# Block inverse of a delta-rule kernel: an order for its four float16 conversions on ScalarE

## The chip, the cores and the metric

The kernel runs on one core of a Trainium2 chip. The time is the device time of one execution in microseconds, from the first to the last instruction with what the launch adds around it; the numbers of a comparison are medians of several runs. A core has TensorE for matrix products (PE in the profile), VectorE (DVE), ScalarE (ACT), GpSimd (POOL), and SyncE (SP), which issues transfers. ScalarE and GpSimd issue transfers too, each from its own queue (ACTq, POOL).

## The reference

One inference step of a mixer with three branches (a bidirectional gated DeltaNet, a spatial-gating MLP, a Fourier mixer) over 128 context tokens and 2048 latent tokens. What matters here is the DeltaNet. Cut to that:

```python
m = eye + bc[..., :, None] * jnp.einsum('bnhik,bnhjk->bnhij', kc, kc) * dec_strict
rhs = jnp.concatenate([vc * bc[..., None], kc * (bc * jnp.exp(gam))[..., None]], axis=-1)
sol = lax.linalg.triangular_solve(m, rhs, left_side=True, lower=True, unit_diagonal=True)
u0, w = sol[..., :DV], sol[..., DV:]
...
def step(s, inp):
    u0_, w_, qk_, qg_, kd_, gl_ = inp
    u = u0_ - jnp.einsum('bhck,bhkv->bhcv', w_, s)
    o = jnp.einsum('bhck,bhkv->bhcv', qg_, s) + jnp.einsum('bhij,bhjv->bhiv', qk_, u)
    s = gl_[..., None, None] * s + jnp.einsum('bhck,bhcv->bhkv', kd_, u)
    return s, o
```

The matrix m of each chunk is triangular with ones on its diagonal. The kernel inverts it: 32 by 32 blocks on the diagonal first (the block inverse), and from them larger blocks by products.

## The kernel before, in words

The tokens lie in 17 chunks of 128 (chunk 16 is the context). PE's products are made of float16 pairs, a high and a low half of each operand, hence three products for one. Wherever a float32 tile becomes such a pair, ScalarE writes the high half (a Copy with a scale) and VectorE the low half (scaled value minus high half).

Two streams of work are written into one another. The main stream goes through the branches' projections, gates and mixers and gives PE most of its work. The second stream is a Python generator, `delta()`, which the main stream steps along by `pace.tick` and `pace.part` (lines 410 to 450): one step for each 1.6 us of the main stream's matrix work. `delta()` first prepares all chunks and makes the block inverses, then runs the scan, the serial part over 2 x 17 chunks.

The preparation, `prep` (line 1007), goes through seven steps for each chunk: keys made unit length (sums of squares on ScalarE, L1022), queries (L1041) and values (L1036), the transposed keys T (L1050), two steps with the products of keys (L1064 to L1069), two with the products of queries and keys (L1080 to L1083). Each step that makes a float16 tile hands its store to `late` (line 988), which issues it from ScalarE's queue one such step afterwards (L998). `late` also issues, with each such step, one transfer from the list `extra` (L1003).

The chunks form five groups: chunk 16 alone, then four groups of four. `base_inverse(g)` (line 1092) inverts the 32 by 32 blocks of a whole group at once, in one tile with the blocks on the partitions. It is stepped after each preparation step of the following group, so that inverse g runs beside the preparation of group g + 1; the fifth runs alone, after all preparation. It loads the blocks (L1103) into the two halves X and tmp of the tile XB, runs 31 elimination steps that alternate between VectorE (L1114) and GpSimd (L1115) on the tile E, and then writes the result as float16 pairs back into XB, in four parts: two halves j0 of the columns, each in two layouts w. For each part there is one conversion on ScalarE (L1122), the low half on VectorE (L1123) and a `yield`. After each half its two stores to memory (tensor `ei`) follow: in the first four inverses they are put on the list `extra`, so that `late` issues them from ScalarE's queue (two that are left after the fourth go to SP's, L1431); in the fifth one goes to SP's queue (L1130) and one to ScalarE's (L1131).

With eight empty steps at its beginning and fifteen for the elimination, the four conversions of inverses one to four are written behind the third, fourth, fifth and sixth step of the last chunk of the group in preparation, with the main stream's instructions between them as its pace brings it.

The scan's `level` loads `ei` (L1171) and other tiles (L1175, L1177), and its first product is PE's first on the tiles ES and N. The tiles of the scan take the place of the tiles of the preparation in on-chip memory (`dl.close()`, then a new pool), so that they can be written only once the last stores out of XB have landed.

The order of the instructions on each engine is not the written order. It is planned when the kernel is built: a list scheduler goes through the instructions by a model of their times and lets each engine take what is ready. The hardware then runs each engine's list in that order. Where the written code wants a certain order, it says `issue_after(ins)`: the instructions in that block come behind `ins` in their engine's list. This is an order only, with no semaphore. `queued()` of the engine wrapper does this with the newest instruction that has been written so far for that engine; transfers that the engine issues count among them. Before the change it is used in two places, both on VectorE (L1106 and L1356):

```python
def queued(self):
    e = self.engine.engine
    newest = next((i for i in reversed(self.tc.nc.cur_bb.bb.instructions) if i.engine == e), None)
    return ExitStack() if newest is None else self.tc.issue_after(newest)
```

Of the kernel before, what the change touches and what calls it, by code (L numbers as in the profile page):

```python
# [14 lines left out]
AF = mybir.ActivationFunctionType  # L15
# [20 lines left out]
FS = 4096.0  # L36
# [158 lines left out]
def hybrid_flow_kernel(ctx: ExitStack, tc: tile.TileContext, x_prompt, x_sample, state_delta, c, c_ctx, w_ada,  # L195
# [4 lines left out]
    G, V, A, PE = [_InTurn(tc, e_) for e_ in (nc.gpsimd, nc.vector, nc.scalar, nc.tensor)]  # L200
# [9 lines left out]
    def sb(pl, shape, tag, dt=F32, bufs=None):  # L210
        kw = {} if bufs is None else {"bufs": bufs}
        return pl.tile(list(shape), dt, tag=tag, name=nm(tag), **kw)
# [190 lines left out]
    def getw(n=1, ahead=0):  # L403
        i = wnext[0]
        wnext[0] += n
        fetch(i + n)
        while len(wdone) - len(wsteps) < i + n:
            weight_step()
        fetch(i + n + ahead)
        r = wdone[i:i + n]  # L410
        return r[0] if n == 1 else r
# [519 lines left out]
    for ct in range(12):  # L931
        w = getw(1, 2 if ct < 6 else min(4, 15 - ct))
# [159 lines left out]
    def base_inverse(g):  # L1092
        nt = len(GROUPS[g])
        nb = 16 * nt
        XB = sb(dq, [P, 2048], "XB")
        X, tmp = XB[:, 0:1024], XB[:, 1024:2048]
        E = sb(dq, [P, 1024], "E")
        if nt < 4:
            V.memset(X, 0.0)
            V.memset(tmp, 0.0)  # L1100
        b3 = lambda t_: t_.rearrange("p (j i) -> p j i", j=32)
        for d in range(2):
            SY.dma_start((X if d == 0 else tmp)[64 * d:64 * d + nb, :], ndD[g][d].rearrange("t h (b j) i -> (t h b) (j i)", b=4))  # L1103
        for _ in range(8):
            yield 0
        with V.queued():  # L1106
            V.tensor_copy(b3(X[64:P, :]), tmp[64:P, :].rearrange("p (i j) -> p j i", j=32))
        G.memset(E, 0.0)
        G.memset(E[:, 0:1024:33], 1.0)
        X3, E3 = b3(X), b3(E)  # L1110
        for k in range(31, 0, -1):
            n_ = 32 - k
            t3 = tmp[:, 0:k * n_].rearrange("p (j i) -> p j i", j=k)
            V.tensor_tensor(t3, X3[:, 0:k, k:k + 1].to_broadcast([P, k, n_]), E3[:, k:k + 1, k:32].to_broadcast([P, k, n_]), ALU.mult)  # L1114
            G.tensor_tensor(E3[:, 0:k, k:32], E3[:, 0:k, k:32], t3, ALU.subtract)  # L1115
            if k % 2 == 0:
                yield 1
        both = XB.bitcast(F16).rearrange("p (j l w c) -> p j l w c", j=32, l=2, w=2)
        for j0 in (0, 16):
            js = slice(j0, j0 + 16)  # L1120
            for w, src in ((0, E3), (1, E.rearrange("p (i j) -> p j i", j=32))):
                A.activation(both[:, js, 0, w, :], src[:, js], AF.Copy, scale=FS)  # L1122
                V.scalar_tensor_tensor(both[:, js, 1, w, :], src[:, js], FS, both[:, js, 0, w, :], ALU.mult, ALU.subtract)  # L1123
                yield 1
            out = [(eD[g][d][js].rearrange("j t (y x) -> (t y) j x", x=128),
                    both[64 * d:64 * d + nb, js].rearrange("p j l w c -> p j (l w c)")) for d in range(2)]
            if g < 4:
                extra.extend(out)
            else:
                SY.dma_start(*out[0])  # L1130
                A.dma_start(*out[1])  # L1131
# [278 lines left out]
    def delta():  # L1410
# [5 lines left out]
        for i_, (g, ci, t) in enumerate(seq):  # L1416
            if ci == 0 and g:
                for r_ in base:
                    if r_:
                        yield 1  # L1420
                base = base_inverse(g - 1)
            for n_, _ in enumerate(prep(g, ci, t, seq[i_ + 1][2] if i_ < 16 else None, held)):
                yield 1
                if next(base, 0):
                    yield 1
# [6 lines left out]
        for _ in base_inverse(4):  # L1432
            yield 1
# [757 lines left out]
```

## Time and profile before

| | |
|---|---|
| median of 3 runs | 2145.91 us (2145.07 to 2146.69) |
| the profiled execution | 2150.07 us |
| its span, first to last instruction | 2148.3 us |
| mean granted clock of TensorE | 0.992 |
| PE busy | 2085.2 us (97%) |
| ScalarE busy | 1060.8 us (49%) |
| VectorE busy | 1327.9 us (62%) |
| GpSimd busy | 843.3 us (39%) |

A row of a timeline gives the start in us from the span's start, the time it took, the engine, the line, the operation, the tiles (written<-read) and how many instructions are merged into the row; in square brackets stands how long the engine was idle before it and what ended that. A row of the chain gives start, time and what the chain went through. A row of stretches gives the stretch, its length, the busy time of PE, PE's weight loads, VectorE, ScalarE and GpSimd with the number of instructions, then the granted clock (1.00 is full), the share of the DMA engines and GB/s. ACTq and SPq are instructions that the engine only issues or waits in, such as DMA issues.

### The profile page before, as it was taken

The numbers are of one execution on the slowest core, as the hardware profiler recorded it, in microseconds if no ns is written. First come the engines' busy times: TensorE is split into PE (matmuls) and PEld (weight loads), VectorE is DVE, ScalarE is ACT, GpSimd is POOL, SyncE is SP. The second block draws the span as 40 slices with busy tenths as digits, with TensorE's granted clock in tenths as the row PEclk, the third lists the DMA queues.
The fourth block names the chain that finished last, engine by engine and source line by source line (L and its number), as shares of the span: only waits on it lengthen the run. The fifth ranks groups of instructions, "written<-read, shape, count | busy, mean of one in ns | idle before, by whom it ended". The sixth has DMA issues, their size and how long they took to land.

```text
span 2148.3 us, 42630 instructions
## 1 busy us (share of the span) xinstructions
PE 2085.2 (97%) x16133; PEld 1196.8 (56%) x16133; DVE 1327.9 (62%) x2945; ACT 1060.8 (49%) x2457; POOL 843.3 (39%) x1089
## 2 busy tenths in 40 slices
PE   7999999999999999989899999999999999999997
PEld 4454444455555677777555556565655444444443
DVE  6656854388777786456655555766665564666245
ACT  5554744475656664445544445665653353453112
POOL 0321332225565555542321233354542234333464
PEclk9999999999999999999999999999999999999999
DMA  9525722277877743444655555867664655456852
GB/s 353 219 77 189 267 102 102 74 223 226 259 228 246 225 138 93 121 132 138 205 182 161 167 162 184 258 206 232 210 204 127 209 167 173 167 198 240 335 220 89
DMA packets 222910, 403.25 MB, mean 188 GB/s; under 512 B 39720, under 2 KB 109632, under 8 KB 219888
## 3 DMA queue, kind: packets, MB, share of 16 engines
q1 hardware_dynamic: 167664, 290.84, 42.5%
q0 software_dynamic: 15216, 65.89, 8.2%
q10 hardware_dynamic: 39824, 43.79, 6.0%
q8 instruction: 127, 2.08, 0.4%
q14 instruction: 79, 0.65, 0.1%
HBM read 258.19 MB, written 142.24 MB: 186 GB/s over the span
## 4 chain that ended last, share of the span: by engine, by line
PE 70%; DVE 9%; DMA 9%; ACT 4%; POOL 4%; issue 3%; SPq 1%; ACTq 0%; DVEq 0%; POOLq 0%
PE b L250 66%; PE b L182 4%; DMA st<-br 2%; POOL E L1115 1%; DMA pa<-pa 1%; DMA wst<-in_w_blk_dram 1%; DVE XB L1114 1%; POOL st L1466 1%; DMA ab<-in_w_adb_dram 1%; PE b L1016 1%; DMA sqk<-qk 1%; DMA ei<-XB 0%; ACT xh L182 0%; ACT nd L1066 0%; DVE XB L1123 0%
## 5 line engine op out<-in xcount | busy, mean ns | idle before, releaser
L250 PE MATMUL b<-xh,whi 128*128 128x512 f16 (+1 forms) x1920 | 651.1, 348 | 2.8 <-DVE sg L1456 1.8
L250 PE MATMUL b<-xl,whi 128*128 128x512 f16 (+1 forms) x1920 | 651.2, 348 | 0.0
L250 PE MATMUL b<-xh,wlo 128*128 128x512 f16 (+1 forms) x1920 | 650.1, 347 | 0.0
L250 PEld LDWEIGHTS <-whi 128*128 128x128 f16 x3856 | 352.7, 98 | 326.4 <-issue 7.3
L250 PEld LDWEIGHTS <-wlo 128*128 128x128 f16 x1928 | 188.8, 98 | 176.1 <-issue 2.2
L250 PE MATMUL b<-big,bhi 128*128 128x512 f16 (+1 forms) x960 | 252.3, 347 | 1.9 <-ACT big L1699 1.1
L250 PE MATMUL b<-big,blo 128*128 128x512 f16 (+1 forms) x480 | 163.1, 347 | 0.0
L1743 POOL TENSOR_TENSOR mrow<-mrow,sg 128x512 f32<-128x512 f32 (+1 forms) x80 | 94.4, 1182 | 131.2 <-DVE sg L1742 99.5
L953 POOL TENSOR_TENSOR cy<-cy,raw 128x545 f32<-128x545 f32 (+1 forms) x48 | 65.8, 1395 | 181.8 <-ACT raw L952 181.8
L250 PEld LDWEIGHTS <-xh 128*128 128x128 f16 x1496 | 116.9, 98 | 28.8 <-issue 1.4
L250 PEld LDWEIGHTS <-bhi 128*128 128x128 f16 x960 | 87.7, 98 | 78.1 <-issue 2.6
L1115 POOL TENSOR_TENSOR E<-E,XB 128x31 f32<-128x31 f32 (+15 forms) x155 | 94.1, 607 | 85.7 <-DVE XB L1114 68.8
L250 PEld LDWEIGHTS <-xl 128*128 128x128 f16 x1068 | 98.1, 98 | 44.8 <-DMA tw<-tw 1.4
L1733 ACT ACTIVATE sg<-b,winv 128x512 f32<-128x512 f32 (+1 forms) x120 | 73.9, 616 | 87.1 <-PE b L250 86.4
L1188 POOL COPY T<-ES 32x256 f16<-32x256 f16 x68 | 31.8, 467 | 188.6 <-DMA ES<-ei 167.9
L250 PE MATMUL b<-whi,xh 128*128 128x128 f16 x544 | 92.8, 219 | 0.0
L250 PE MATMUL b<-whi,xl 128*128 128x128 f16 x544 | 92.8, 219 | 0.0
L250 PE MATMUL b<-wlo,xh 128*128 128x128 f16 x544 | 92.8, 219 | 0.0
L328 DVE SCALAR_TENSOR_TENSOR wlo<-wst,wsc,whi 128x1024 f16<-128x1024 f32 x52 | 71.1, 1368 | 33.1 <-ACT whi L327 32.7
L315 ACT ACTIVATE wlo<-wst 128x1024 f16<-128x1024 f32 x52 | 54.9, 1055 | 54.5 <-DMA wst<-in_w_blk_dram 51.2
L1114 DVE TENSOR_TENSOR XB<-XB,E 128x31 f32<-128x31 f32 (+15 forms) x155 | 55.2, 356 | 41.8 <-POOL E L1115 41.2
L1295 POOL TENSOR_TENSOR skn<-skn,ed 128x512 f32<-128x512 f32 x34 | 37.7, 1109 | 109.7 <-DMA skn<-kv 109.7
(532 smaller groups left out, 4317.9 us busy)
## 6 DMA issues: line engine op xcount, KB each, us to landing
wst<-in_w_blk_dram SPq DMA_DIRECT2D x58, 512.0 KB, 4.5
pa<-pa POOLq DMA_DIRECT2D x16, 896.0 KB, 4.4
qkv<-cy POOLq DMA_DIRECT2D x12, 1089.0 KB, 5.3
st<-br SPq DMA_DIRECT2D x48, 256.0 KB, 3.2
mrow<-mrg SPq DMA_DIRECT2D x16, 576.0 KB, 4.6
pa<-pa SPq DMA_DIRECT2D x5, 1792.0 KB, 17.3
dc<-dec SPq DMA_DIRECT2D x17, 512.0 KB, 4.8
kq<-qkv SPq DMA_DIRECT2D x34, 256.0 KB, 4.5
```

The costliest lines, as they stand in the source:

```text
L182: self.last = f(*args, **kw)
L250: newest[0] = PE.matmul(out, l, r, start=start, stop=stop, skip_group_check=reopened)
L315: w.squared = A.activation(w.lo, st, AF.Square, accum_out=ss)
L328: w.low = V.scalar_tensor_tensor(w.lo, st, s, w.hi, ALU.mult, ALU.subtract)
L953: G.tensor_tensor(y[:, c0:c1], y[:, c0:c1], raw[:, 1 + c0:1 + c1], ALU.mult)
L1016: PE.transpose(ps[:, hs(h)], cur[part][:, h, :], ident)
L1114: V.tensor_tensor(t3, X3[:, 0:k, k:k + 1].to_broadcast([P, k, n_]), E3[:, k:k + 1, k:32].to_broadcast([P, k, n_]), ALU.mult)
L1115: G.tensor_tensor(E3[:, 0:k, k:32], E3[:, 0:k, k:32], t3, ALU.subtract)
L1188: G.tensor_copy(T16[rows(a0, b), :, :, b], ES[0:32, :, 2 * a0 + b, :, wT])
L1295: G.tensor_tensor(h3(kn_), h3(kn_), bc(ed[:, d, t, :], P), ALU.mult)
L1733: gated_[0] = A.activation(sg, ps, AF.Sigmoid, scale=gw.inv)
L1743: G.tensor_tensor(mr, mr, sg, ALU.add)
```

## The change

Each of the four conversions is put under `A.queued()`: it comes behind the newest instruction written for ScalarE at that point. Nothing is added to or taken from the work.

```diff
@@ -1119,7 +1119,8 @@
         for j0 in (0, 16):
             js = slice(j0, j0 + 16)
             for w, src in ((0, E3), (1, E.rearrange("p (i j) -> p j i", j=32))):
-                A.activation(both[:, js, 0, w, :], src[:, js], AF.Copy, scale=FS)
+                with A.queued():
+                    A.activation(both[:, js, 0, w, :], src[:, js], AF.Copy, scale=FS)
                 V.scalar_tensor_tensor(both[:, js, 1, w, :], src[:, js], FS, both[:, js, 0, w, :], ALU.mult, ALU.subtract)
                 yield 1
```

## The prediction

> **What bounds the kernel now.** I read the page's busy shares first, then the chain of waits piece by piece around the block inverses, then ScalarE's and VectorE's timelines at each inverse, and last the busy time by stretch. Of the page:
>
> ```profile
> span 2148.3 us, 42630 instructions
> PE 2085.2 (97%) x16133; PEld 1196.8 (56%) x16133; DVE 1327.9 (62%) x2945; ACT 1060.8 (49%) x2457; POOL 843.3 (39%) x1089
> ```
>
> TensorE (PE) is busy 2085 of 2148 us, so a change on ScalarE (ACT, 49%) counts only where PE stands still, or where it runs at a lower clock. The line of the diff runs twenty times, and each conversion is followed by its low half on VectorE (DVE):
>
> ```profile
> L1122 ACT ACTIVATE XB<-E x20: 612/846/1112, 548.1 to 881.0; 128x512 f16<-128x512 f32 x20
> L1123 DVE SCALAR_TENSOR_TENSOR XB<-E,XB x20: 671/1031/1485, 552.4 to 882.3; 128x512 f16<-128x512 f32 x20
> ```
>
> That is five inverses of four conversions: 20 x 0.85 = 17 us of ACT in all. No instruction and no byte is added or removed; what moves is the order. Where this order lies on the path is told by the pieces of the chain between the fourth inverse and the first product of the scan:
>
> ```profile
> 817.72 2.03 ACT XB L1122 x3
> 819.77 2.78 DVE XB L1123 x3
> ...
> 823.32 5.18 DMA ei<-XB
> ...
> 829.29 5.19 DMA XB<-nd
> ...
> 874.28 2.37 DMA br<-st
> ...
> 879.10 1.52 ACT XB L1122 x2
> ...
> 883.33 5.41 DMA ei<-XB
> ...
> 899.12 1.72 DMA N<-n
> ```
>
> The reader is to see one serial line: conversions of the fourth inverse, their stores, the loads of the fifth inverse into the same tile, its 31 elimination steps, its conversions, its stores, and then the loads that the scan starts with. At the end of it PE stands and waits, and the stretch behind it is the poorest one of the middle of the run (PE's row, then the stretches: wall time, PE busy, ..., granted clock):
>
> ```profile
> 901.10 0.18 PE L250 MATMUL b<-ES,N 128*128 128x32 f16 x1 [1.95 <-DMA N<-n]
> ```
>
> ```profile
> 895.00:901.00 6.00, 3.72 (x30) 1.87 (x27) 4.43 (x12) 4.47 (x9) 2.54 (x4) 1.00 0.58 154
> 901.00:907.00 6.00, 5.90 (x29) 2.71 (x30) 1.60 (x4) 1.82 (x4) 3.64 (x6) 0.72 0.53 169
> 907.00:914.00 7.00, 4.46 (x28) 1.99 (x27) 2.15 (x5) 1.37 (x4) 1.98 (x4) 1.00 0.27 83
> 914.00:925.00 11.00, 9.51 (x103) 7.64 (x104) 7.01 (x19) 5.02 (x14) 4.47 (x11) 0.69 0.28 79
> 925.00:940.00 15.00, 12.74 (x202) 10.86 (x199) 10.24 (x25) 7.61 (x21) 5.37 (x10) 1.00 0.58 161
> ```
>
> Idle: 2.28 + 0.10 + 2.54 + 1.49 + 2.26 = 8.67 us. Lost to the clock: 6 x 0.28 + 11 x 0.31 = 1.7 + 3.4 = 5.1 us. So 13.8 us of these 45 are not work.
>
> **Which conversions move at all.** In the written order the conversions stand behind the third, fourth, fifth and sixth step of the preparation of a group's last chunk. The new edge makes each wait its turn behind the newest ScalarE instruction written before it, a DMA issue on that queue included. In inverses one to four the first three conversions already run long after those instructions (in the first, all of that chunk's preparation on ScalarE is done before 548). So three of four edges hold already and cost nothing. The edge that bites is the fourth conversion's: in inverses one to three the newest instruction is the issue of the first half's store (L1003), in the fourth it is the square of the 128-token unit (L1467), and in the fifth it is the store L1131 already for the third. A store of the first half is issued only when the second low half is done, so ScalarE now waits for VectorE between conversions.
>
> **Inverses one to three.** The timelines of ScalarE, then VectorE for the first, then ScalarE for the second and third, then the stretches of the latter two:
>
> ```profile
> 548.06 3.09 ACT L1122 ACTIVATE XB<-E 128x512 f16<-128x512 f32 x4 [0.53 <-POOL E L1115]
> ...
> 554.85 2.54 ACTq L1003 DMA_DIRECT2D ei<-XB  x3
> 557.43 0.60 ACT L1050 ACTIVATE T<-b 128x512 f16<-128x512 f32 x1 [3.36 <-DVE XB L1123]
> ```
>
> ```profile
> 555.40 1.65 DVE L1123 SCALAR_TENSOR_TENSOR XB<-E,XB 128x512 f16<-128x512 f32 x2
> ```
>
> ```profile
> 632.47 1.63 ACT L1122 ACTIVATE XB<-E 128x512 f16<-128x512 f32 x2
> 633.69 0.67 ACTq L1003 DMA_DIRECT2D ei<-XB  x1
> ```
>
> ```profile
> 721.68 1.61 ACT L1122 ACTIVATE XB<-E 128x512 f16<-128x512 f32 x2
> 723.88 0.66 ACTq L1003 DMA_DIRECT2D ei<-XB  x1
> ```
>
> ```profile
> 625.00:650.00 25.00, 25.00 (x192) 15.14 (x190) 17.29 (x40) 17.56 (x50) 10.59 (x17) 1.00 0.86 253
> 710.00:735.00 25.00, 25.00 (x145) 13.08 (x143) 17.60 (x39) 15.07 (x42) 12.40 (x20) 1.00 0.69 214
> ```
>
> First: the conversion goes behind the issue at 554.85. With 0.67 us for the issue (the second's row) and 0.61 for the conversion (the shortest of L1122) it ends at 556.13, and its low half (0.67 to 1.03) at 556.8 to 557.2, against 555.40 + 1.65 = 557.05 now. The conversion T, which waits 3.36 us behind the stores in ScalarE's queue, and PE's products of T behind it, come 0.25 us earlier to 0.5 us later (0.15, and 0.35 more if an eviction gets in between). I take +0.2. Second and third: the fourth conversion slips from an end at 634.10 to 634.97 (633.69 + 0.67 + 0.61), and from 723.29 to 725.15: 0.9 and 1.9 us. Behind it wait its low half and the second half's stores, which nobody reads before the scan. PE is busy 25.00 of 25.00 us in both stretches, and this covers it: 0, and at worst these 0.9 + 1.9 us if the cover were gone.
>
> **Inverse four.** ScalarE, then VectorE:
>
> ```profile
> 817.61 3.11 ACT L1122 ACTIVATE XB<-E 128x512 f16<-128x512 f32 x4
> 820.63 0.62 ACT L1467 ACTIVATE sg<-st 128x512 f32<-128x512 f32 x1
> ...
> 821.24 0.29 ACT L1467 ACTIVATE sg<-st 128x128 f32<-128x128 f32 x1
> ```
>
> ```profile
> 818.36 4.18 DVE L1123 SCALAR_TENSOR_TENSOR XB<-E,XB 128x512 f16<-128x512 f32 x4
> ```
>
> Four low halves in 4.18 us are 1.05 each, so the fourth starts at 821.49. The conversion now goes behind both squares. If these move up into its place (0.7 us earlier), it ends at 821.5 and VectorE loses nothing. If they can't, it starts at 821.53, ends at 822.14, and the low half is 0.65 late. The store, the load of the fifth inverse and its 31 steps follow; a step late in these steps can vanish in the wait for the store at 874.28, on which GpSimd's work beside the steps hangs. Between 0 and 0.65, I take 0.3.
>
> **Inverse five.** ScalarE, then VectorE:
>
> ```profile
> 879.00 3.12 ACT L1122 ACTIVATE XB<-E 128x512 f16<-128x512 f32 x4
> 881.72 0.60 ACTq L1131 DMA_DIRECT2D ei<-XB  x1
> 882.02 0.57 ACT L1571 ACTIVATE xc<-b 128x512 f16<-128x512 f32 x1
> ```
>
> ```profile
> 880.63 1.65 DVE L1123 SCALAR_TENSOR_TENSOR XB<-E,XB 128x512 f16<-128x512 f32 x2 [0.30 <-ACT XB L1122]
> ```
>
> The second low half ends at 880.63 + 0.83 = 881.46 and the store is issued at 881.72. Now two conversions stand behind it: 881.72 + 0.60 + 2 x 0.61 = 883.54, then the fourth low half at 0.67 to 1.03, so the second store leaves at 884.2 to 884.6, not 883.33: 0.9 to 1.2 us late. If the eviction xc (0.57) also gets in between, up to 1.8. I take 1.4. Nothing hides it. The scan's tiles lie where the store reads, so GpSimd clears them only then:
>
> ```profile
> 889.13 0.95 POOL L1137 MEMSET R<- 128x1024 f16 x1 [9.39 <-DMA ei<-XB]
> ```
>
> The loads and PE at 901.10 hang on the same end, and PE's gap of 1.95 grows to about 3.6 with the fourth inverse's share.
>
> **The clock behind the gap.** The shown stretches price it: after 1.95 us of idling PE loses 1.7 us to the clock (901 to 907), after the 2.54 us that stand idle in 907 to 914 it loses 3.4. A gap of 3.6 is nearest to the second, so 3.4 - 1.7 = +1.7; the bounds are 0 and 3.4. [...]
>
> **The sum.** 0.2 + 0.3 + 1.4 + 1.7 = +3.6 us. The profiled execution took 2150.07 us, 1.8 more than its span, and is 4.2 above the median of the shown runs; on the profile's own base the new time is 2153.7, and against the median 2145.91 + 3.6 = 2149.5. The lower bounds add up to -0.25 + 0.9 = +0.65, the upper ones to 0.5 + 2.8 (cover gone) + 0.65 + 1.8 + 3.4 = +9.15: 2146.6 to 2155.1.
>
> **The rivals.**
> 1. *Nothing bites.* Three edges in four hold already, and the rest is hidden: PE's order is drawn up anew at the build, with main products put into the gap at 901. For it: PE's 25.00 of 25.00 in two of the five places. Against it: the fifth inverse's store, which has no cover in the trace. Time 2145.9, at most 1.5 off.
> 2. *Faster: the later start is filled.* The order of every engine behind 821 is planned anew with later inputs, and main products go where PE now idles between 895 and 940. There are 13.8 us there; half of it is 6.9, less the 1.9 us of delay: -5.0, so 2140.9. For it: PE waits there for loads (1.95 on N) while another stage has matrix products in hand. Against it: nothing in the edit asks for it, and the planner had the same chance before. It decides if PE's gap before the first product of the scan goes below 1 us.
> 3. *Slower: the scan is what sets the end.* The same planning puts one more product group ahead of the scan's first one. Such a group is 24 products of 512 columns, and the spacing of their starts is (550.22 - 549.14) / 5 = 0.216 us, from the first and the last of six in a row:
>
> ```profile
> 549.14 0.38 PE L250 MATMUL b<-xl,whi 128*128 128x512 f16 x1
> ...
> 550.22 0.38 PE L250 MATMUL b<-xh,whi 128*128 128x512 f16 x1
> ```
>
> So 5.2 us. The scan then starts 1.7 + 5.2 = 6.9 us later and, being serial, ends as much later; where the last branch waits for it this is paid in full: 2152.8. For it: in the stretches from 895 to 940 PE already waits for the scan's steps. Against it: a later stretch in which PE hardly waits:
>
> ```profile
> 1100.00:1300.00 200.00, 199.57 (x1833) 119.27 (x1832) 108.51 (x293) 88.10 (x206) 53.13 (x86) 1.00 0.54 165
> ```
>
> It decides when the last scan tile comes after the products that can be done without it.
>
> **How the numbers follow.** Two measurements of this kernel can be told apart from about 0.2%, or 4.3 us: faster is below 2141.6, slower above 2150.2. The forecast has 0.45; its own range, 2147 to 2152, is cut by the upper bound, 0.25 of it to "same" and 0.20 to "slower". Rival 1 has 0.10, all "same". Rival 2 has 0.23, and rival 3 has 0.22. That gives faster 0.23, same 0.35, slower 0.42. The range goes from 2140 to 2157: down to rival 2's time, and up past the bounds' 2155 by rival 3 with part of the clock's price.
>
> **What would show it.** Right: in the first four inverses three conversions in a row and the fourth behind a store or a square; in the fifth L1131 between the second and third; its second store at 884.2 to 885.2 after a start as now; PE's gap before the first product of ES and N at 3 to 4 us; a clock below 0.72 in the six us behind it. Wrong: that gap at 2 us or less, or gone; conversions spread over the preparation's steps (then the written order is not where I put it); a difference of more than 3 us that arises before 800, where I have only 0.2; or PE's idle time behind 940 changed by more than the sum.

## The result and the profile after

The changed kernel takes 2152.79 us (median; 2150.82 to 2154.68), the kernel before in the same comparison 2145.74 (2140.25 to 2148.55). The ratio is 1.0033, with a 95% interval of 1.0022 to 1.0045: 7.1 us slower, between 4.7 and 9.7. The forecast was 2149.5, in a range of 2140 to 2157.

The two profiled executions must be read with care. That of before took 2150.07 us, more than any of its runs in this comparison; that of after took 2150.84, near its own lowest. They differ by 0.8 us where the medians differ by 7. So the totals of the two profiles can't be subtracted. What can be compared is the order of instructions, single waits, and distances from a fixed point.

In the changed kernel every line behind 1121 has a number higher by one: the conversion is L1123, its low half L1124, the fifth inverse's stores L1131 and L1132, the main stream's conversions L1572 and L1573. The experiments keep the numbers of before.

The page after:

```profile
span 2149.1 us, 42632 instructions
PE 2088.6 (97%) x16133; PEld 1199.8 (56%) x16133; DVE 1331.9 (62%) x2945; ACT 1062.0 (49%) x2457; POOL 843.0 (39%) x1089
```

ScalarE's timeline after, at the first, second and third inverse:

```profile
548.03 2.12 ACT L1123 ACTIVATE XB<-E 128x512 f16<-128x512 f32 x3 [0.53 <-POOL E L1115]
...
554.80 0.33 ACTq L1003 DMA_DIRECT2D ei<-XB  x1
...
555.18 1.08 ACT L1123 ACTIVATE XB<-E 128x512 f16<-128x512 f32 x1 [1.14 <-DVE XB L1124]
...
557.73 0.60 ACT L1050 ACTIVATE T<-b 128x512 f16<-128x512 f32 x1 [1.47 <-DVE XB L1124]
...
634.87 1.10 ACT L1123 ACTIVATE XB<-E 128x512 f16<-128x512 f32 x1
...
723.58 1.34 ACTq L1003 DMA_DIRECT2D ei<-XB  x2
...
724.56 1.10 ACT L1123 ACTIVATE XB<-E 128x512 f16<-128x512 f32 x1
```

Three conversions run at once and the fourth waits behind an issue of a store, as forecast. The conversion T starts at 557.73 instead of 557.43, 0.3 us late; the fourth conversions of the other two now stand at 634.87 and 724.56.

At the fourth and the fifth inverse, ScalarE's timeline, then VectorE's, then SyncE's:

```profile
810.00 1.15 ACT L1123 ACTIVATE XB<-E 128x512 f16<-128x512 f32 x2
...
816.00 1.05 ACT L1123 ACTIVATE XB<-E 128x512 f16<-128x512 f32 x1
816.95 0.58 ACT L1572 ACTIVATE xc<-b 128x512 f16<-128x512 f32 x1
818.14 2.45 ACTq L1003 DMA_DIRECT2D ei<-XB  x2
820.63 0.63 ACT L1468 ACTIVATE sg<-st 128x512 f32<-128x512 f32 x1 [3.10 <-issue]
...
821.55 1.07 ACT L1123 ACTIVATE XB<-E 128x512 f16<-128x512 f32 x1
...
878.57 1.62 ACT L1123 ACTIVATE XB<-E 128x512 f16<-128x512 f32 x2
...
881.96 0.61 ACTq L1132 DMA_DIRECT2D ei<-XB  x1
882.62 1.62 ACT L1123 ACTIVATE XB<-E 128x512 f16<-128x512 f32 x2 [1.06 <-DVE XB L1124]
...
885.34 0.59 ACTq L1132 DMA_DIRECT2D ei<-XB  x1
```

```profile
822.66 1.05 DVE L1124 SCALAR_TENSOR_TENSOR XB<-E,XB 128x512 f16<-128x512 f32 x1 [3.96 <-ACT XB L1123]
...
884.26 1.04 DVE L1124 SCALAR_TENSOR_TENSOR XB<-E,XB 128x512 f16<-128x512 f32 x1 [0.29 <-ACT XB L1123]
```

```profile
823.74 1.37 SPq L1432 DMA_DIRECT2D ei<-XB  x2
```

In the fifth, L1132 (formerly L1131) stands between the second and the third conversion, and the second store is issued at 885.34 instead of 883.33. In the fourth the new order goes further than forecast. The first three conversions no longer stand in a row: two run at 810.00, the third at 816.00. Two issues of stores hold ScalarE's queue for 2.45 us from 818.14, the squares L1468 stand behind them, and the last conversion stands behind both. Its low half starts at 822.66; in before it started at 821.49.

PE, at its first product on ES and N, and as a fixed point ahead of the fourth inverse's conversions the transposes L1049 of the preparation's last chunk but one (after):

```profile
767.77 0.61 PE L1049 MATMUL b<-cst,tok 128*128 128x128 f32 x4
...
902.27 0.18 PE L250 MATMUL b<-ES,N 128*128 128x32 f16 x1 [2.55 <-POOL T L1189]
```

The gap ahead of the scan has grown from 1.95 to 2.55 us, not to 3.6, and its start from 901.10 to 902.27. The six microseconds behind it ran at full clock (a stretch of after):

```profile
901.00:907.00 6.00, 4.73 (x36) 2.52 (x37) 3.35 (x8) 2.94 (x5) 3.50 (x7) 1.00 0.48 124
```

And there is a wait of PE that the forecast doesn't have. ScalarE's timeline after, then VectorE's and PE's, at the load of the fifth inverse:

```profile
827.72 0.60 ACT L1572 ACTIVATE xc<-b 128x512 f16<-128x512 f32 x1 [1.51 <-PE b L250]
```

```profile
834.18 1.03 DVE L1107 COPY XB<-XB 64x1024 f32<-64x1024 f32 x1 [6.65 <-DMA XB<-nd]
835.24 0.69 DVE L1573 SCALAR_TENSOR_TENSOR xc<-b,xc 128x512 f16<-128x512 f32 x1
```

```profile
835.99 0.77 PE L250 MATMUL b<-cf,xc 128*128 128x128 f16 x10 [2.23 <-DVE xc L1573]
```

VectorE stands idle for 6.65 us in front of the copy L1107, which opens the fifth inverse and waits for its load. Behind the copy in VectorE's list stands the low half of a tile of the main stream, xc, and PE waits for that. ScalarE had begun the high half of this tile at 827.72, so what keeps the low half is its place in the list. In the kernel before, it stands ahead of the copy:

```profile
829.16 0.69 DVE L1572 SCALAR_TENSOR_TENSOR xc<-b,xc 128x512 f16<-128x512 f32 x1 [1.87 <-ACT xc L1571]
829.83 0.69 DVE L1572 SCALAR_TENSOR_TENSOR Y<-b,Y 128x512 f16<-128x512 f32 x1
834.50 1.05 DVE L1107 COPY XB<-XB 64x1024 f32<-64x1024 f32 x1 [3.97 <-DMA XB<-nd]
```

The copy waits there too, but what PE wants next is done before it. The stretches around this place, of before and then of after, say what this costs in these two executions:

```profile
768.00:828.00 60.00, 56.55 (x675) 44.40 (x674) 46.68 (x114) 35.24 (x92) 33.95 (x54) 0.97 0.40 126
828.00:836.00 8.00, 8.00 (x147) 8.00 (x145) 2.62 (x4) 2.39 (x4) 0.07 (x1) 1.00 0.49 136
836.00:844.00 8.00, 8.00 (x56) 4.20 (x54) 5.44 (x20) 3.63 (x6) 4.07 (x10) 1.00 0.00 1
844.00:860.00 16.00, 14.87 (x142) 9.61 (x141) 12.18 (x28) 5.02 (x14) 10.71 (x17) 1.00 0.10 34
```

```profile
768.00:828.00 60.00, 57.45 (x689) 45.13 (x688) 47.09 (x113) 35.22 (x92) 34.45 (x52) 0.97 0.41 125
828.00:836.00 8.00, 5.77 (x105) 5.60 (x102) 1.79 (x4) 1.51 (x3) 0.00 (x0) 1.00 0.52 136
836.00:844.00 8.00, 8.00 (x65) 5.75 (x66) 4.36 (x14) 2.51 (x5) 3.94 (x9) 0.79 0.01 3
844.00:860.00 16.00, 15.90 (x124) 9.21 (x122) 12.24 (x31) 5.74 (x13) 9.85 (x16) 1.00 0.11 34
```

From 828 to 844 PE was busy throughout at full clock; now it idles 2.23 us and then loses 8 x 0.21 = 1.7 to the clock. The stretches on both sides give 0.90 and 1.03 of idle time back. Net: 2.0 us lost ahead of the fifth inverse's end, in a stretch from which the forecast took nothing but its 0.3 for a late load.

### The profile page after: what moved, and what is told of

Same layout as the page of the kernel before. It is cut to its first block, busy times and chain, and to the rows that moved or that the text cites. A ratio compares the mean times of both kernels' runs of the same rounds, so it can differ in the third digit from the quotient of the medians.

```text
span 2149.1 us, 42632 instructions
## 1 busy us (share of the span) xinstructions
PE 2088.6 (97%) x16133; PEld 1199.8 (56%) x16133; DVE 1331.9 (62%) x2945; ACT 1062.0 (49%) x2457; POOL 843.0 (39%) x1089
## 4 chain that ended last, share of the span: by engine, by line
PE 45%; DMA 7%; DVE 7%; ACT 3%; POOL 3%; issue 2%; SPq 0%; ACTq 0%; POOLq 0%; DVEq 0%
PE b L250 44%; DMA st<-br 2%; DMA pa<-pa 1%; POOL E L1115 1%; DMA wst<-in_w_blk_dram 1%; DVE XB L1114 1%; POOL st L1467 0%; DMA ei<-XB 0%; DMA ES<-ei 0%; DVE sg L476 0%; ACT of L1376 0%; ACT big L1700 0%; DMA wst<-in_w_ada_dram 0%; DVE big L1701 0%; PE b L1383 0%
```

## The experiments

Two theories stood against each other. The first is that of the forecast: a chain of late stores (inverses four and five), paid at the start of the scan. The second: the edges make the planner draw up the rest of the program anew, and the loss lies in the new order, wherever it is worst. All experiments are the kernel before with the edit in some of the five inverses (g = 0 to 4), or with one thing more. All ratios stand against the kernel before on the same chip (one chip for e1 to e4, one for e5 to e8, one for e9 to e12), with 95% intervals. They are not the quotients of the two medians, which lie up to 0.0013 away (e9: 1.0032).

| run | edges in inverses | ratio | interval | median us, before |
|---|---|---|---|---|
| e1 | all but each one's last (fifth: last two) | 0.9999 | 0.9989 to 1.0009 | 2147.38, 2147.43 |
| e8 | one | 0.9994 | 0.9982 to 1.0007 | 2146.98, 2146.88 |
| e7 | two | 1.0003 | 0.9992 to 1.0015 | 2148.50, 2146.88 |
| e3 | three | 1.0002 | 0.9992 to 1.0011 | 2146.84, 2147.43 |
| e2 | four, five | 1.0000 | 0.9989 to 1.0011 | 2148.25, 2147.43 |
| e6 | one to three | 1.0012 | 1.0000 to 1.0024 | 2148.03, 2146.88 |
| e4 | all but three | 1.0016 | 1.0005 to 1.0027 | 2150.14, 2147.43 |
| e9 | three to five | 1.0019 | 1.0008 to 1.0031 | 2152.34, 2145.51 |
| e5 | all (the change again) | 1.0024 | 1.0014 to 1.0033 | 2151.65, 2146.88 |
| e10 | all, fifth's copy L1107 on GpSimd | 1.0005 | 0.9993 to 1.0017 | 2148.18, 2145.51 |
| e11 | none, fifth's copy L1107 on GpSimd | 0.9993 | 0.9981 to 1.0005 | 2145.58, 2145.51 |
| e12 | none, last conversion of the fifth nine times | 1.0045 | 1.0032 to 1.0058 | 2155.96, 2145.51 |

**Which edges do anything.**

```diff
-A.activation(both[:, js, 0, w, :], src[:, js], AF.Copy, scale=FS)
+with A.queued() if (g < 4 and (j0, w) != (16, 1)) or (g == 4 and j0 == 0) else ExitStack(): A.activation(both[:, js, 0, w, :], src[:, js], AF.Copy, scale=FS)
```

> The order is asked only of the first three conversions of inverses one to four and of the first two of the fifth. Set side by side, every engine's list is that of the kernel before, instruction for instruction. Both theories (late stores of inverses four and five; a new plan behind inverse three): ratio 1.000, inside +-0.1%, about 2146 us. Anything beyond that is what two loadings of one program differ by, and the scale for the other runs. Its profile is a second execution of the plan before: the stall before 550 to 553 us and the wait before the scan's first product stay, the clock's half-speed pieces may fall elsewhere.

The lists of instructions of all five engines are those of the kernel before, and the trace has each engine's instructions in the same order; the time is the same: 0.9999. These fourteen of the twenty edges do nothing. The whole change is in six: the last conversion of each inverse, and in the fifth the one before it too. This run also gives a second profile of the old order, and its span is 2143.1 us, 5.2 shorter than that of before with the same lists.

**One part at a time.** The conditions are `g == 0`, `g == 1`, `g == 2` and `g > 2`:

```diff
-A.activation(both[:, js, 0, w, :], src[:, js], AF.Copy, scale=FS)
+with A.queued() if g > 2 else ExitStack(): A.activation(both[:, js, 0, w, :], src[:, js], AF.Copy, scale=FS)
```

> The order is asked in inverse one alone. Only ScalarE's list differs, in 12 lines: the fourth conversion goes behind the first two stores. If the local wait carries it: the values' and keys' next steps start 0.3 us or more later and the ratio is 1.0005 to 1.002. As predicted: +0.2 us, ratio 0.9995 to 1.0005.

> The order is asked in inverse two alone; PE's list differs in 259 lines between 630 and 760 us. If inverse two carries what all but three showed: ratio 1.001 to 1.0025. If not: 0.999 to 1.001, and inverse one is left.

> The order is asked in inverse three alone; the lists of all engines differ from before in many places behind it (PE 2256 lines). Theory 1: PE is fully busy around this inverse, so nothing, ratio 0.999 to 1.001. Theory 2: the new plan carries the change, ratio 1.002 to 1.0045, +4 to +9 us, with a stall of PE between 800 and 900 us that before does not have.

> The order is asked in inverses four and five alone; PE's list differs from before in 24 lines. Theory 1 (late stores, as predicted): the first product on ES and N comes 1 to 2 us later than before, gap 3 us, and the time carries nearly all of the change, +4 to +7 us, ratio 1.002 to 1.0033. Theory 2 (the plan behind inverse three): the same 1 to 2 us later start, but the time is only +1 to +2 us, ratio below 1.001.

No part alone can be told from the kernel before: each interval holds 1 and reaches 1.5 to 4 us to either side. Both theories miss here: the first expected at least 1.002 of e2, the second of e3. The lists of instructions tell more than the times. The edge in inverse one alone moves 12 lines of ScalarE's list and nothing else. That in two changes 259 lines of PE's list, those in four and five 24. The single edge in inverse three changes 2256 lines: one conversion that comes 2 us later there makes the planner order the rest of the preparation anew, and the scan's beginning too. Compared place by place in the traces, PE's products in after differ from those in before at 1083 places between 643 and 1088 us, and 806 of these lie behind 900 (one product moved shifts all up to its new place). With the late stores of four and five alone the scan does start later (below), and yet this costs too little to be seen in that run.

**Several parts together.** The conditions are `g < 3`, `g != 2`, `g > 1` and, for the change again, `True`:

```diff
-A.activation(both[:, js, 0, w, :], src[:, js], AF.Copy, scale=FS)
+with A.queued() if g > 1 else ExitStack(): A.activation(both[:, js, 0, w, :], src[:, js], AF.Copy, scale=FS)
```

> The order is asked in inverses one to three, where the prediction saw +0.2 us. Additive parts: as all but three less four and five plus three, ratio 1.001 to 1.002. Theory 1 (late stores of four and five): ratio 0.999 to 1.001. Theory 2 (a stall that comes only with all): ratio 0.999 to 1.001, no stall at 834.

> The order is asked in all inverses but the third; PE's list differs from before in 283 lines. Theory 1: as the change, ratio 1.002 to 1.004. Theory 2: as inverses four and five alone, ratio below 1.001, and no stall of PE at 834 us.

> The order is asked in inverses three, four and five. PE's list is that of the whole change but for 259 lines around inverse two. By the profiles so far (nothing lost before 768 us, 7 us between 768 and 972 in the whole change, 3 to 4 in the parts): ratio 1.002 to 1.0033, the stall at 834 us again, the first product on ES and N 2 us late against a fixed point before inverse four. By adding up the times of the parts measured so far (some 2 us from one and two, 1 from three, 2 from four and five): ratio 1.0005 to 1.0018.

> The change itself once more, with its two lines on one, beside the other parts of this call. If the first comparison's +0.33% stands: ratio 1.0022 to 1.0045. If it was high by chance (the parts so far give 0.00% for inverses four and five, 0.02% for three, 0.16% for all but three): ratio 1.0005 to 1.002. Theory 2, a stall of its own at 834 us that only the whole change has: the profile shows it again, 2 us, with a piece of half clock behind it.

The change again is slower again, by 1.0024, or 3.0 to 7.1 us. Inverses three to five give 1.0019 of it; PE's list there differs from that of the whole change only in the 259 lines of inverse two. All but three give 1.0016, one to three 1.0012. So no single edge carries the loss: each combination shows a part of it, and within these intervals (2 us and more to each side) the parts may add up or not. That three to five carry most of it is the best reading of e9, but e4 and e6 keep it from being all.

The traces of the three profiled executions with the new order (after, e5, e9) agree on two places, and the old order's don't have the first. PE's timeline in e5, then in e9, at 834:

```profile
836.61 1.25 PE L250 MATMUL b<-cf,xc 128*128 128x128 f16 x10 [2.68 <-DVE xc L1572]
```

```profile
835.55 0.85 PE L250 MATMUL b<-cf,xc 128*128 128x128 f16 x10 [2.28 <-DVE xc L1572]
```

The stall behind the copy stands in all three, with 2.23 to 2.68 us. It isn't in before, e1 or e8, and not in e2, e4 or e7. In e3 and e6 there are shorter ones (1.42 us; 1.47 and 1.41). So it comes with the new order behind inverse three, and has its full length with the edges of four and five besides.

The other place is the start of the scan. From the transposes L1049 at 768 (767.93 in before, 767.77 in after) to the first product on ES and N it is 133.2 us in before, 132.2 in e1, 132.3 in e7 (whose products behind 713 us stand in the old order) and 131.2 in e8; with the new order it is 134.5 in after, 134.6 in e5 and 134.4 in e9. The means are 132.2 and 134.5: 2.3 us later. With the edges of four and five alone, in e2 and e4, it is 133.9 and 133.6.

**What a late start costs.** To price it by itself, the last conversion of the fifth inverse is run nine times in the kernel before (each time with the same values), which delays its second store and nothing ahead of it:

```diff
-A.activation(both[:, js, 0, w, :], src[:, js], AF.Copy, scale=FS)
+for _ in range(9 if g == 4 and (j0, w) == (16, 1) else 1): A.activation(both[:, js, 0, w, :], src[:, js], AF.Copy, scale=FS)
```

> The kernel before, with the last conversion of inverse five written nine times (the same values; ScalarE does eight more conversions, about 8 x 0.6 = 4.9 us, ahead of the last low half and store). Theory 1 (a late second store is paid one for one): the first product on ES and N about 5 us later, +5 to +7 us, ratio 1.0022 to 1.0035. If a late start of the scan is hidden by other products of PE: ratio below 1.001.

```profile
884.26 4.45 ACT L1122 ACTIVATE XB<-E 128x512 f16<-128x512 f32 x4
888.62 0.57 ACT L1571 ACTIVATE xc<-b 128x512 f16<-128x512 f32 x1
889.09 1.07 ACT L1122 ACTIVATE XB<-E 128x512 f16<-128x512 f32 x1
...
893.87 0.59 ACTq L1131 DMA_DIRECT2D ei<-XB  x1
```

```profile
768.15 0.61 PE L1049 MATMUL b<-cst,tok 128*128 128x128 f32 x4
...
910.01 0.45 PE L250 MATMUL b<-ES,N 128*128 128x32 f16 x8 [3.30 <-POOL T L1188]
```

ScalarE's timeline of this run and then PE's: the planner put the main stream's work between the repeats, so that the store went out at 893.87, 10.5 us later than in before, and the scan started 141.9 us behind the transposes, 9.7 later than in the old order; 5 were expected. The time rose by the same amount: 1.0045, that is 9.7 us (6.9 to 12.4). In this run the late start is paid one for one, as far as the interval can say. PE wasn't idle all that time, for it waited only 3.30 us; main products ran until then, and were missing behind the start (PE busy 0.94 of 7.00 us, in before 4.46):

```profile
907.00:914.00 7.00, 0.94 (x16) 0.69 (x16) 1.82 (x5) 2.25 (x7) 3.52 (x7) 0.84 0.60 164
```

The mean granted clock of this kernel's runs fell to 0.9885, from 0.9914 in the kernel before, by my estimate 0.0029 x 2150 = 6 us of the loss; so by it a good part of this run's loss is the clock's; that the wait brought this about is not shown. The changed kernel's runs have 0.9910, against 0.9911 to 0.9914: less than 1 us.

The other runs don't make a rule of it. The scan has 34 levels (2 x 17 chunks), and each opens with eight products on ES and N. These are the distances in us from the transposes at 768 to the first level and to the ninth:

| runs | first level | ninth level |
|---|---|---|
| before, e1, e7, e8 | 133.2, 132.2, 132.3, 131.2 | 285.2, 281.9, 281.2, 279.6 |
| after, e5, e9 | 134.5, 134.6, 134.4 | 286.1, 291.8, 286.1 |
| e2, e4 | 133.9, 133.6 | 285.5, 283.8 |
| e3, e6 | 124.6, 127.1 | 282.3, 286.2 |
| e10, e11 (below) | 135.0, 136.8 | 278.6, 277.2 |
| e12 | 141.9 | 292.5 |

PE's rows for e3 (transposes at 768.27), then for e11 (at 769.91):

```profile
892.84 0.45 PE L250 MATMUL b<-ES,N 128*128 128x32 f16 x8 [2.29 <-DMA N<-n]
...
1050.55 0.26 PE L250 MATMUL b<-ES,N 128*128 128x32 f16 x4
```

```profile
906.67 0.18 PE L250 MATMUL b<-ES,N 128*128 128x32 f16 x1 [0.56 <-POOL T L1188]
...
1047.10 0.26 PE L250 MATMUL b<-ES,N 128*128 128x32 f16 x4
```

With another order of PE's products, a scan that starts 7.6 us early (e3) is no further at the ninth level, and one that starts 4.6 us late (e11) has made up for it; their times are 1.0002 and 0.9993. From the ninth level to the end every run takes 1091.6 to 1097.6 us, whatever its edges. So where the first level stands doesn't settle the time; the order of the products of the first eight levels counts as well. The change is 2.3 us late at the first level and 6.0 at the ninth, by the means of its three executions and of the four of the old order. Within one order the ninth levels lie up to 5.7 us apart, so the second figure is rough.

**The stall behind the copy.** The copy at the fifth inverse's beginning goes to GpSimd, in the changed kernel and, as a control, in the kernel before:

```diff
-with V.queued():
-    V.tensor_copy(b3(X[64:P, :]), tmp[64:P, :].rearrange("p (i j) -> p j i", j=32))
+with V.queued() if g < 4 else ExitStack():
+    (V if g < 4 else G).tensor_copy(b3(X[64:P, :]), tmp[64:P, :].rearrange("p (i j) -> p j i", j=32))
```

> The whole change, and in the fifth inverse the copy of the second half of the blocks (L1107) on GpSimd, not on VectorE, where it stands ahead of the main stream's low half xc and waits for the load XB<-nd. Theory 2 (that wait is what the whole change has and its parts have not): no stall of PE at 834, 2 to 4 us less than the change, ratio to before 1.000 to 1.0015. Theory 1 (late stores and the clock): still 1.002 to 1.003.

> The control to the run with the change: the kernel before with the same copy on GpSimd. Where the copy stalls nothing, as in the profile before: ratio 0.999 to 1.001. If it helps by itself: below 0.999, and then the gain in the other run is not the change's stall.

```profile
828.00:836.00 8.00, 8.00 (x135) 7.53 (x133) 1.13 (x2) 1.60 (x3) 1.85 (x1) 1.00 0.48 132
836.00:844.00 8.00, 6.18 (x38) 2.93 (x37) 5.16 (x20) 3.58 (x6) 4.13 (x10) 1.00 0.01 4
```

```profile
839.01 0.73 PE L250 MATMUL b<-cf,xc 128*128 128x128 f16 x10 [1.82 <-DVE xc L1572]
```

These are the stretches of e10 and PE's timeline. With the edges, the time goes to 1.0005 instead of the change's 1.0024 and 1.0033; without them the copy's move is worth 0.9993, nothing that can be seen. The best reading is that most of the loss goes away when the copy leaves VectorE, though the intervals of e10 and e5 overlap. But the trace doesn't bear out the simple reason: a wait for xc is still there, 1.82 us instead of 2.23 to 2.68 and some 3 us later, and it is the clock that stays at 1.00 in this execution. The scan still starts late: 135.0 us behind the transposes. The move changed the planned order once more, behind the scan's start too (its ninth level stands at 278.6), and how much of the gain belongs to the shorter stall isn't shown.

## Why the prediction came out right, and which steps failed

**Right: slower, and within the range.** The time lies 3.3 us above the forecast, and rival 3 gave the very number, 2152.8, by another mechanism: a whole product group ahead of the scan, 6.9 us late. The scan starts 2.3 us later, so that it wasn't this; that the number agrees is luck. Rivals 1 and 2 fall too: the comparison's interval excludes no change and any gain.

**Right: three edges in four do nothing in inverses one to four, and the fifth's first two do nothing.** e1 has the old lists, engine by engine.

**Right: inverse one.** T came 0.30 us late, between the bounds -0.25 and 0.5; its edge alone gives 0.9994. And nothing of size arises before 768, as forecast; the stretch from 430 to there, in before, then after:

```profile
430.00:768.00 338.00, 333.61 (x2550) 202.37 (x2548) 264.39 (x652) 211.56 (x646) 179.60 (x259) 1.00 0.74 233
```

```profile
430.00:768.00 338.00, 334.26 (x2547) 202.72 (x2546) 265.52 (x653) 211.24 (x647) 181.44 (x260) 0.99 0.74 232
```

PE's busy time differs by 0.65 us of 338, and the transposes at its end stand at 767.77 instead of 767.93.

**Right in mechanism, short in size: the late stores.** The forecast had 0.3 from the fourth inverse and 1.4 from the fifth, 1.7 in all. The fourth's low half was 1.17 us late (822.66 against 821.49, and its store 823.74 against 822.57), above the bound of 0.65; the squares that the forecast let move up stood behind 2.45 us of issues instead. More than half of this vanished on the way: from the transposes at 768, the first conversion of the fifth starts at 110.8 to 111.3 us in the three executions of the new order and at 110.2 to 111.1 in the four of the old one, 0.5 later by the means. The fifth's second store went out at 885.34, 2.0 us late and just past the 885.2 that I gave; by the same means it is 3.0 late. So the fifth gave some 2.5 us where the forecast had 1.4. The start of the scan is 2.3 us later. That this much is paid to the end is not shown: e12 shows it for four times the delay, while e2 starts 1.7 late and has a ratio of 1.0000, with an interval that reaches 2.4 us.

**Failed: "PE is busy 25.00 of 25.00 us in both stretches, and this covers it: 0".** Of the time in that stretch this was true, and for inverse two nothing speaks against it. Of the program it was false for inverse three: the edge's effect didn't end at the stores that nobody reads, it went through the planner into 2256 lines of PE's list. Rivals 2 and 3 have a new plan in them, but only at the scan; I looked for it nowhere else. Together with the edges of four and five this put a low half of the main stream behind a copy that waits for a load, and PE waits there 2.23 to 2.68 us, in all three executions of the new order and in none of the old one. Net of what the neighbouring stretches give back this wait is 2.0 us in after against before. That the runs lose as much by it is argued from the traces and from e10, not shown. The new plan reaches into the scan's first eight levels as well, and there the rest of the delay at the ninth level arises.

**Failed: the clock term, +1.7 behind the gap at 901.** The gap grew to 2.55, not 3.6, and the six us behind it ran at 1.00, not below 0.72. What the forecast read as the price of a gap belongs to one execution: the stretches of before that lost 1.7 and 3.4 us did so in that execution, while e1, with the same lists, was granted 0.98 from 895 to 1000 instead of 0.95 (after has 0.95 as well):

```profile
895.00:1000.00 105.00, 96.43 (x1327) 76.01 (x1324) 62.45 (x159) 51.82 (x129) 43.23 (x71) 0.98 0.46 137
```

Over the runs the changed kernel's mean clock is as before (0.9910, against 0.9911 to 0.9914).

**The sum after the fact.** The two comparisons of this order have 7.1 us (4.7 to 9.7) and 5.2 (3.0 to 7.1). The traces have 2.3 at the start of the scan and 6.0 at its ninth level, so by these means the loss is there by then, and more than half of it arises where the forecast had only the clock's 1.7. The clock can't be much of it: between the two levels it takes 9.1 us in the new order and 8.5 in the old, by the means. The 2.0 us that PE loses around 834 lie in the same stretch as the 2.3, and no run shows that the two add up. The right sign came partly from a wrong term, since without the 1.7 of the clock the forecast would have been +1.9, inside what can't be told from no change.

**Open.** How the six edges share the loss: the single runs are all within their error, and the combinations show that there is more than one place (e4 is at 1.0016 without the stall at 834). Whether the copy's place alone causes what three to five add. And which of the products in the scan's first eight levels stand in the way: no run changed their order alone.

## What to carry to other kernels

An order "behind the newest instruction of this engine" counts DMA issues as well, and here such an issue waited for its data: behind L1132 in ScalarE's list, the conversion at 882.62 came after 1.06 us of idle time that VectorE's low half ended (the 0.61 of the issue is in it), although no data of the conversion asks for it. In a program whose order is planned at the build, an edge has no local price: compare the two lists of instructions engine by engine first, and look wherever they differ for an instruction that waits for a load ahead of one that TensorE needs, far from the edited line too. Don't take the start of a serial stage for its end either: see where its later steps stand. Don't subtract two profiles to find a few us: measure from a fixed point ahead of the change, and require that a wait is there in every execution of the one order and in none of the other.

## What the runs showed of the hardware

The same lists of instructions, executed twice, gave spans of 2148.3 (before) and 2143.1 us (e1), and single runs of the kernel before went from 2140.25 to 2148.55 in one comparison. The granted clock did not fall at all the same places in the two executions, before and after: from 901 to 907 it was 0.72 in before and 1.00 in after, although PE's wait ahead of it was longer in after (2.55 against 1.95 us). The 2.23 us ahead of 835.99 in after were followed by 0.79 (836 to 844), the 1.82 ahead of 839.01 in e10 by 1.00 up to 860. In before the clock was 0.50 from 902.0 to 905.4 and from 915.7 to 922.5, in after from 836.6 to 840.0, which makes the 0.72 over 6 us and the 0.79 over 8. So in these executions waits of PE of about 2 us came ahead of a lower clock in some places and not in others, and one profile can't price them. Over the runs the mean clock fell by 0.003 in e12, where the wait ahead of the scan was 3.30 us, and moved by 0.001 at most in the others. And two DMA issues held ScalarE's queue for 2.45 us at 818.14 in after (0.62 and 1.79), where the single issues in the rows shown took 0.33 to 0.67; no trace shows why.
